# A 31-tap convolution split over three engines, and four FFN tiles per block in another matrix form

## The chip, the cores and the metric

The kernel runs on one core of one Trainium2 chip. Its time is device microseconds of one execution, 2560.61 in the median of three runs before the change (2559.72 to 2563.85). Times in this document are in microseconds (us) unless marked ns. Engines have the profile's names: PE is TensorE (matrix products), DVE is VectorE, ACT is ScalarE, POOL is GpSimd, SP issues the DMAs.

## The reference, cut to what matters

Two residual layers over a sequence of 1024 tokens of width 1024, in float32: a state-space mixer and an FFN, then a causal convolution module and an FFN, then a norm.

```python
def conformer_conv_module(u, w_pw1, b_pw1, dw_w, dw_b, ln_g, ln_b, w_pw2, b_pw2):
    h = u @ w_pw1 + b_pw1
    a, g = jnp.split(h, 2, axis=-1)
    h = a * jax.nn.sigmoid(g)
    h = causal_depthwise_conv(h, dw_w, dw_b)
    h = jax.nn.silu(layernorm(h, ln_g, ln_b))
    return h @ w_pw2 + b_pw2

def swiglu_ffn(u, w_gate, w_up, w_down):
    return (jax.nn.silu(u @ w_gate) * (u @ w_up)) @ w_down
```

The depthwise convolution has 31 taps for each of 1024 channels. An FFN has a hidden width of 2816: 22 tiles of 128.

## The kernel before

Activations stand transposed, 128 channels on the partitions and tokens along the free dimension. The tokens are worked in two blocks of 512, b = 0 and 1. Products are exact to about float32 by splitting each operand: `split` (L200) writes a rounded high half on ACT (L201) and the remainder as a low half on DVE or, where `self.weng` says so, on POOL (L202). `gemm` (L222) then makes three products for each 128 rows of the contraction, low by high, high by low, high by high, 512 columns each (L226). A gate, an up and a pw1 unit contract over 1024, so each is 24 products.

`weight` (L204) brings a unit's weights by one DMA into one of two staging buffers (`wst`) and splits them in two halves of 4 x 128 columns, `whi` and `wlo`, each with four buffers: two units' worth. ACT fills a `whi` when PE has released the one that stood there, and the engine of the low half follows it.

An FFN tile can also be made in the seven-product form (`seven`, L709): the gate (or up) of a pair of tiles is a 2 x 2 block product of which seven instead of eight block products are made, from sums of weight blocks and of activation blocks; each is 4 x 3 products of 256 columns (L758). The sums and the splits are on DVE and ACT.

`run` writes the order of the work as a list of units. Around each block's convolution, a phase goes like this: the norm of the block; then 16 pw1 units (`pw1`, two per tile of 128 channels, one for a and one for g), of which every second ends with a sigmoid on ACT (L946), a gating multiply on DVE (L947) into `ci`, which has 30 columns in front for the tokens before, and in block 0 a copy of the last 30 columns on POOL (L950, the halo of block 1); beside and after them the convolution, one unit per tile (`conv31`); then plain FFN tiles of the other block, in two groups of seven, as matrix work during which the convolution is finished; and, placed between the last of these, the layer norm (`cnorm`) and after it pw2. From the beginning of pw1 to the end of the FFN groups, POOL makes the low halves of the weights (`phase(6, nc.gpsimd)`). The rest of the other block's FFN follows in the seven-product form (`chain7`).

A convolution tile before: one multiply with the bias (L969) and 30 multiply-adds on DVE (L972 in block 0, L974 in block 1), accumulated in a PSUM bank, and in block 0 a copy to SBUF on ACT (L977).

The units' order gives priorities, and a scheduler that runs before the program does makes of it one fixed order of instructions for each engine; `conv31` lowers its own priority by 1000 or 1200, so that its instructions stand behind the units near them. Every engine works its own order strictly from front to back and waits where an operand or a buffer is not ready.

Of the kernel before, what the change touches and what calls it, by code (L numbers as in the profile page):

```python
# [10 lines left out]
AF = mybir.ActivationFunctionType  # L11
ALU = mybir.AluOpType
# [28 lines left out]
BOOST = 60  # L41
NR = 2
HALO = 30
TW = HALO + T
HT = T // 2
MM = 0.2315
# [24 lines left out]
class Unit:  # L71
# [3 lines left out]
    def __init__(self, run, load=None, t=0.0, pre=()):  # L75
        self.run, self.load, self.t, self.pre, self.then = run, load, t, pre, None
# [13 lines left out]
def put(q, *at):  # L90

    out = []
    for i in range(len(q) + 1):
        for k, units in at:
            if (k if k >= 0 else len(q) + k) == i:
                out += units
        out += q[i:i + 1]
    return out


def at(units, places):

    return [(p, units[i:i + 1] if i < len(places) - 1 else units[i:]) for i, p in enumerate(places)]


class Trunk:
# [73 lines left out]
    def halves(self):  # L180
# [4 lines left out]
        self.spare = cp.tile([P, 1], F32, name="spare")  # L185
        self.halo = cp.tile([P, 8, HALO], F32, name="halo")
        o = PAR_OFF["gate"]
# [286 lines left out]
    def in_proj(self, i, u=None, fac=None):  # L474
# [12 lines left out]
        def run(n):  # L487
# [9 lines left out]
            else:  # L497
# [3 lines left out]
                self.nc.scalar.activation(s, acc, AF.Tanh, scale=0.5)  # L501
                self.nc.vector.scalar_tensor_tensor(s, s, 1.0, acc, op0=ALU.add, op1=ALU.mult)
        units = [Unit(lambda n=n: run(n), lambda n=n: load(n)) for n in range(10)]
        if u is not None:
            return [Unit(lambda n=n: gemm(n), lambda n=n: load(n)) for n in range(NR)], [
# [417 lines left out]
    def cin(self, j):  # L923

        return self.ci[j // 3].rearrange("p a t -> p (a t)")[:, j % 3 * TW:(j % 3 + 1) * TW]

    def pw1(self, b):
        nc = self.nc
        W = {}

        def load(j, s):
            W[j, s] = self.weight(self.io["w_pw1"][j, :, s], 8)

        def run(j, s):
            W["acc", s] = self.bank2()
            self.gemm(W["acc", s], W.pop((j, s)), self.U[b])
            if s == 0:
                return
            if j % 3 == 0:
                self.ci.append(self.big.new("ci"))  # L940
            x = self.cin(j)
            dst = x[:, HALO:]
            if b == 1:
                nc.gpsimd.tensor_copy(x[:, :HALO], self.halo[:, j])
            t = self.small.new("sig")
            nc.scalar.activation(t, W.pop(("acc", 1)), AF.Sigmoid, bias=self.pcol("b_pw1", 8 + j))  # L946
            nc.vector.scalar_tensor_tensor(dst, W.pop(("acc", 0)), self.pcol("b_pw1", j), t, op0=ALU.add, op1=ALU.mult)  # L947
            self.small.drop(t)
            if b == 0:
                nc.gpsimd.tensor_copy(self.halo[:, j], x[:, T:])  # L950
            if j == 7:
                self.big.drop(*self.UB.pop(b))
        return [Unit(lambda j=j, s=s: run(j, s), lambda j=j, s=s: load(j, s), 24 * MM)
                for j in range(8) for s in range(2)]

    def conv31(self, b, delay):

        nc, tc = self.nc, self.tc

        def tile_(j):  # L960
            keep = tc.cur_priority
            tc.cur_priority = keep + delay
            if j % 4 == 0:
                self.co[b].append(self.big.new("co"))
            c = self.co[b][j // 4][:, j % 4]
            x = self.cin(j)
            w = lambda s: self.pcol("dw_w", 31 * j + 30 - s)
            acc = self.bank("cv")
            nc.vector.tensor_scalar(acc, x[:, HALO:], w(0), self.pcol("dw_b", j), op0=ALU.mult, op1=ALU.add)  # L969
            for s in range(1, 31):  # L970
                if b == 0:
                    nc.vector.scalar_tensor_tensor(acc[:, s:], x[:, HALO:TW - s], w(s), acc[:, s:], op0=ALU.mult, op1=ALU.add)  # L972
                else:
                    nc.vector.scalar_tensor_tensor(acc if s < 30 else c, x[:, HALO - s:TW - s], w(s), acc,  # L974
                                                   op0=ALU.mult, op1=ALU.add)
            if b == 0:
                nc.scalar.activation(c, acc, AF.Copy)  # L977
            if j == 7:
                self.big.drop(*self.ci)
                self.ci = []  # L980
            tc.cur_priority = keep
        return [Unit(lambda j=j: tile_(j)) for j in range(8)]
# [80 lines left out]
    def run(self):  # L1063
        nc = self.nc
# [40 lines left out]
        fast = lambda *a, **k: self.ffn(*a, fast=True, **k)  # L1105
# [3 lines left out]
        c = self.chain7(fast(0, 0, 6, [0]), fast(0, 6, 6, [0]), fast(0, 12, 4, [0]), fast(0, 16, 2, [0], [0]), free=0, hold=5)  # L1109
        q += [call(self.phase7)] + put(c, *at(n1, (-11, -9, -7, -5, -3))) + [call(self.phase, 8)]  # L1110
        n0 = self.norm_u(0, "cv_norm")
        p1, cv = self.pw1(0), self.conv31(0, 1000)
        c = self.chain(self.ffn(0, 8, 7, [1]), self.ffn(0, 15, 7, [1]))
        q += put(c[:2], *at(n0, (0, 1))) + [call(self.phase, 6, nc.gpsimd)]
        for j in range(8):
            q += p1[2 * j:2 * j + 2] + (cv[j:j + 1] if j < 4 else [])
# [2 lines left out]
        q += [call(self.phase, 8)]  # L1119
        q += put(p2, *at(self.sums_u(1), (2, 3, 4, 5, 6)))  # L1120
        n0 = self.norm_u(0, "ffn_norm", 8)
        c = self.chain7(fast(0, 0, 6, [1]), fast(0, 6, 2, [1], [1]), free=1, hold=6)
        q += [call(self.phase7)] + put(c, *at(n0, (-13, -11, -9, -7, -5))) + [call(self.phase, 8)]
        n1 = self.norm_u(1, "cv_norm")
        p1, cv = self.pw1(1), self.conv31(1, 1200)
        c = self.chain(self.ffn(1, 0, 7, [0]), self.ffn(1, 7, 7, [0]))
        q += put(c[:2], *at(n1, (0, 1))) + [call(self.phase, 6, nc.gpsimd)]
        for j in range(8):
            q += p1[2 * j:2 * j + 2] + (cv[j:j + 1] if j < 4 else [])
# [3 lines left out]
        self.whole = {1}  # L1133
        q += put(p2, *at(self.sums_u(0), (2, 3, 4, 5, 6)))
        n1 = self.norm_u(1, "ffn_norm", 8, whole=True)
        c = self.chain7(fast(1, 14, 6, [0]), fast(1, 20, 2, [0], [0]), free=0, hold=5)
        q += [call(self.phase7)] + put(c, *at(n1, (-13, -11, -9, -7, -5)))
        f0, f1, f2 = self.final(0), self.final(1, (0,)), self.final(1, (HT,))
        c = self.chain7(self.ffn(1, 0, 2, [1]), fast(1, 2, 6, [1]), fast(1, 8, 6, [1]), fast(1, 14, 4, [1]),
                        fast(1, 18, 4, [1], [1], True), free=1, hold=4)  # L1140
# [104 lines left out]
```

## Time and profile before

| | |
|---|---|
| median of three runs | 2560.61 |
| profiled execution: time, span | 2560.45, 2558.7 |
| granted PE clock, mean over the span | 0.995 |
| `wlo` on POOL (L202) | 232 operations, 303.2 busy |
| multiply-adds of the convolution, L972 and the larger group of L974 | 240 and 232, 160.1 and 158.6 busy |
| block 0: first gating multiply, last multiply-add | 1224.2, 1445.3 |
| block 1: first multiply-add, last | 1727.5, 1949.1 |

A row of the time line has start, length, engine, line, operation, what it writes and reads, and in brackets how long the engine was idle before it and on whom it waited. A row by stretch of time has, for each engine, its busy time and in parentheses the number of its instructions. A row of one line's instructions has the shortest, median and longest duration in ns. A PE product is shown longer than the time after which the next one starts.

### The profile page before, as it was taken

How to read it: one execution, taken by the hardware profiler on the slowest of the kernel's cores; microseconds unless marked ns; L12 is line 12 of the kernel's file. 1: busy time of each engine (PE TensorE's matmuls, PEld its weight loads, DVE VectorE, ACT ScalarE, POOL GpSimd, SP SyncE). 2: the span in 40 equal slices, each digit the busy share in tenths (PEclk: the TensorE clock that was granted, in tenths of full speed). 3: DMA queues.
4: the chain of work that ended last, by engine and by line, in shares of the span. 5: the costliest groups of instructions: out<-in, count | busy, mean ns of one | idle time of the engine just before them, and what ended most of it. 6: DMA issues, size and time to landing. Idle time of an engine off the chain costs nothing. (4 is left out here: it accounts for less than half of the span.)

```text
span 2558.7 us, 35973 instructions
## 1 busy us (share of the span) xinstructions
PE 2516.8 (98%) x13794; PEld 2132.0 (83%) x13794; DVE 2066.5 (81%) x3158; ACT 1224.7 (48%) x2135; POOL 473.7 (19%) x449
## 2 busy tenths in 40 slices
PE   8999999999999999998999999999999999999998
PEld 6787887888887899997888879978888899799997
DVE  7898889888889886768899677589996776996676
ACT  5554565655555454544333364452323554554443
POOL 3213211111111000000544540004444300000000
PEclk9999999999999999999999999999999999999999
DMA  4222222222223223322232333222233322332322
GB/s 144 82 65 74 78 61 75 75 79 71 75 71 103 84 104 100 107 72 79 91 99 91 98 125 103 65 86 94 99 91 97 127 88 88 128 120 93 114 85 71
DMA packets 72316, 233.54 MB, mean 91 GB/s; under 512 B 8016, under 2 KB 14416, under 8 KB 65232
## 3 DMA queue, kind: packets, MB, share of 16 engines
q1 hardware_dynamic: 72144, 231.25, 27.9%
q8 instruction: 108, 1.77, 0.3%
q14 instruction: 64, 0.52, 0.1%
HBM read 227.02 MB, written 4.19 MB: 90 GB/s over the span
## 5 line engine op out<-in xcount | busy, mean ns | idle before, releaser
L201 ACT ACTIVATE whi<-wst 128x512 fp32r<-128x512 f32 (+3 forms) x676 | 402.8, 597 | 815.4 <-PE p L226 657.8
L226 PE MATMUL p<-uhi_b,wlo 128*128 128x512 f32 x1432 | 572.1, 400 | 4.5 <-DVE wlo L202 2.3
L226 PE MATMUL p<-ulo_b,whi 128*128 128x512 f32 x1432 | 562.2, 393 | 3.0 <-DVE ulo_b L202 2.1
L226 PE MATMUL p<-uhi_b,whi 128*128 128x512 f32 x1432 | 562.6, 393 | 0.0
L202 POOL TENSOR_TENSOR wlo<-wst,whi 128x512 fp32r<-128x512 f32 x232 | 303.2, 1308 | 761.0 <-ACT whi L201 760.7
L226 PE MATMUL p<-hid_b,whi 128*128 128x512 f32 x1344 | 420.0, 393 | 2.3 <-DVE hid_b L202 2.3
L202 DVE TENSOR_TENSOR wlo<-wst,whi 128x512 fp32r<-128x512 f32 (+2 forms) x444 | 303.1, 685 | 136.9 <-ACT whi L201 133.5
L226 PEld LDWEIGHTS p<-uhi_b,wlo 128*128 128x128 f32 x1432 | 269.4, 188 | 70.0 <-ACT uhi_b L201 3.8
L226 PEld LDWEIGHTS p<-ulo_b,whi 128*128 128x128 f32 x1432 | 269.4, 188 | 66.5 <-DVE ulo_b L202 3.9
L758 PE MATMUL p<-uhi_b,wh_b 128*128 128x256 f32 x1728 | 322.0, 281 | 0.4 <-DVE wh_b L202 0.4
L226 PEld LDWEIGHTS p<-uhi_b,whi 128*128 128x128 f32 x1432 | 269.3, 188 | 60.4 <-issue 0.2
L226 PEld LDWEIGHTS p<-hid_b,whi 128*128 128x128 f32 x1344 | 252.4, 188 | 57.6 <-DVE hid_b L202 3.2
L758 PEld LDWEIGHTS p<-uhi_b,wh_b 128*128 128x128 f32 x1728 | 272.6, 189 | 2.6 <-DVE wh_b L202 0.6
L226 PE MATMUL p<-hid_b,wlo 128*128 128x512 f32 x672 | 265.7, 395 | 2.4 <-DVE h L862 2.2
L758 PE MATMUL p<-ulo_b,wh_b 128*128 128x256 f32 x864 | 243.0, 282 | 0.0
L758 PE MATMUL p<-tu_b,wh_b 128*128 128x256 f32 x1296 | 170.4, 281 | 0.0
L758 PEld LDWEIGHTS p<-ulo_b,wh_b 128*128 128x128 f32 x864 | 163.7, 190 | 1.9
L758 PEld LDWEIGHTS p<-tu_b,wh_b 128*128 128x128 f32 x1296 | 161.3, 189 | 0.8
L972 DVE SCALAR_TENSOR_TENSOR p<-ci_b,par,p 128x503 f32<-128x503 f32 (+28 forms) x240 | 160.1, 734 | 0.6
L974 DVE SCALAR_TENSOR_TENSOR p<-ci_b,par,p 128x512 f32<-128x512 f32 x232 | 158.6, 748 | 0.5
L201 ACT ACTIVATE wh_b<-ws_b 128x1024 fp32r<-128x1024 f32 x108 | 114.0, 1059 | 87.6 <-PE p L758 37.7
L226 PEld LDWEIGHTS p<-hid_b,wlo 128*128 128x128 f32 x672 | 126.3, 188 | 31.8 <-DVE h L862 4.6
(235 smaller groups left out, 3984.7 us busy)
## 6 DMA issues: line engine op xcount, KB each, us to landing
wq_b<-w_gu SPq DMA_DIRECT2D x54, 1024.0 KB, 4.8
wst<-w_in SPq DMA_DIRECT2D x80, 512.0 KB, 3.5
wst<-w_gu SPq DMA_DIRECT2D x68, 512.0 KB, 3.5
wst<-w_pw SPq DMA_DIRECT2D x48, 512.0 KB, 3.5
wst<-w_dn SPq DMA_DIRECT2D x48, 384.0 KB, 3.1
wst<-w_out SPq DMA_DIRECT2D x64, 256.0 KB, 2.6
wst<-w_dn SPq DMA_DIRECT2D x32, 448.0 KB, 3.3
wst<-w_dn SPq DMA_DIRECT2D x32, 256.0 KB, 2.7
```

The costliest lines, as they stand in the source:

```text
L201: self.nc.scalar.activation(hi, src, AF.Copy)
L202: (eng or self.nc.vector).tensor_tensor(lo, src, hi.bitcast(F32), ALU.subtract)
L226: self.nc.tensor.matmul(acc, a, b, start=n == 0, stop=n == tot - 1)
L758: nc.tensor.matmul(to, x, y, start=n == 0 and not more, stop=n == 11, skip_group_check=True)
L972: nc.vector.scalar_tensor_tensor(acc[:, s:], x[:, HALO:TW - s], w(s), acc[:, s:], op0=ALU.mult, op1=ALU.add)
L974: nc.vector.scalar_tensor_tensor(acc if s < 30 else c, x[:, HALO - s:TW - s], w(s), acc, op0=ALU.mult, op1=ALU.add)
```

## The change

Of a tile's 31 taps, 22 stay on DVE (1 to 22, into PSUM). Tap 0 with the bias becomes an Identity on ACT into the SBUF tile `co`, the remaining eight become scaled copies on ACT into a half-size buffer (`ct`, two places in turn), and POOL adds each to `co` in place. At the end DVE adds its PSUM sum to `co`. In block 0 the first 30 columns of each `ci` are now cleared by POOL instead of being left out.

The FFN tiles beside each convolution become two groups of five instead of two of seven. The four tiles left over join the seven-product part, which gets a further group.

```diff
+NTAP = 23
...
             if b == 1:
                 nc.gpsimd.tensor_copy(x[:, :HALO], self.halo[:, j])
+            else:
+                nc.gpsimd.memset(x[:, :HALO], 0.0)
...
-            nc.vector.tensor_scalar(acc, x[:, HALO:], w(0), self.pcol("dw_b", j), op0=ALU.mult, op1=ALU.add)
-            for s in range(1, 31):
-                if b == 0:
-                    nc.vector.scalar_tensor_tensor(acc[:, s:], x[:, HALO:TW - s], w(s), acc[:, s:], op0=ALU.mult, op1=ALU.add)
-                else:
-                    nc.vector.scalar_tensor_tensor(acc if s < 30 else c, x[:, HALO - s:TW - s], w(s), acc,
-                                                   op0=ALU.mult, op1=ALU.add)
-            if b == 0:
-                nc.scalar.activation(c, acc, AF.Copy)
+            old = lambda k: k if b == 0 else 0
+            nc.vector.tensor_scalar(acc, x[:, HALO - 1:TW - 1], w(1), None, op0=ALU.mult)
+            for k in range(2, NTAP):
+                o = old(k)
+                nc.vector.scalar_tensor_tensor(acc[:, o:], x[:, HALO - k + o:TW - k], w(k), acc[:, o:],
+                                               op0=ALU.mult, op1=ALU.add)
+
+            nc.scalar.activation(c, x[:, HALO:], AF.Identity, scale=w(0), bias=self.pcol("dw_b", j))
+            tmp = self.half.new("ct")
+            for k in range(NTAP, 31):
+                o = old(k)
+                t = tmp.rearrange("p (i a) c -> p i (a c)", i=2)[:, k % 2, o:]
+                nc.scalar.activation(t, x[:, HALO - k + o:TW - k], AF.Copy, scale=w(k))
+                nc.gpsimd.tensor_tensor(c[:, o:], c[:, o:], t, ALU.add)
+            self.half.drop(tmp)
+            nc.vector.tensor_tensor(c, c, acc, ALU.add)
...
-        c = self.chain(self.ffn(0, 8, 7, [1]), self.ffn(0, 15, 7, [1]))
+        c = self.chain(self.ffn(0, 12, 5, [1]), self.ffn(0, 17, 5, [1]))
...
-        c = self.chain7(fast(0, 0, 6, [1]), fast(0, 6, 2, [1], [1]), free=1, hold=6)
+        c = self.chain7(fast(0, 0, 6, [1]), fast(0, 6, 4, [1]), fast(0, 10, 2, [1], [1]), free=1, hold=6)
...
-        c = self.chain(self.ffn(1, 0, 7, [0]), self.ffn(1, 7, 7, [0]))
+        c = self.chain(self.ffn(1, 0, 5, [0]), self.ffn(1, 5, 5, [0]))
...
-        c = self.chain7(fast(1, 14, 6, [0]), fast(1, 20, 2, [0], [0]), free=0, hold=5)
+        c = self.chain7(fast(1, 10, 6, [0]), fast(1, 16, 4, [0]), fast(1, 20, 2, [0], [0]), free=0, hold=5)
```

How the order on the engines changes. POOL, the beginning of block 0's pw1 units, before (`wlo` are the low halves of the weights, `halo` the copies for block 1):

```order
L202 TENSOR_TENSOR wlo_1390_11197<-wst_1388_11194,whi_1389_11196 128x512
L950 COPY halo_174<-ci_b172_11120 128x30
L202 TENSOR_TENSOR wlo_1392_11201<-wst_1388_11194,whi_1391_11200 128x512
L202 TENSOR_TENSOR wlo_1396_11236<-wst_1394_11233,whi_1395_11235 128x512
L202 TENSOR_TENSOR wlo_1398_11240<-wst_1394_11233,whi_1397_11239 128x512
```

The same place now; `co` is the convolution's tile, `ct` the products:

```order
L953 COPY halo_174<-ci_b172_11120 128x30
L985 TENSOR_TENSOR co_b173_11136<-co_b173_11136,ct_x19_11161 128x489
L985 TENSOR_TENSOR co_b173_11136<-co_b173_11136,ct_x19_11161 128x488
L985 TENSOR_TENSOR co_b173_11136<-co_b173_11136,ct_x19_11161 128x487
L203 TENSOR_TENSOR wlo_1392_11211<-wst_1388_11204,whi_1391_11210 128x512
L985 TENSOR_TENSOR co_b173_11136<-co_b173_11136,ct_x19_11161 128x486
L985 TENSOR_TENSOR co_b173_11136<-co_b173_11136,ct_x19_11161 128x485
L985 TENSOR_TENSOR co_b173_11136<-co_b173_11136,ct_x19_11161 128x484
L203 TENSOR_TENSOR wlo_1396_11247<-wst_1394_11244,whi_1395_11246 128x512
L985 TENSOR_TENSOR co_b173_11136<-co_b173_11136,ct_x19_11161 128x483
L985 TENSOR_TENSOR co_b173_11136<-co_b173_11136,ct_x19_11161 128x482
L203 TENSOR_TENSOR wlo_1398_11251<-wst_1394_11244,whi_1397_11250 128x512
```

The eight additions of the first tile stand between the splits of the next two units. The other seven tiles of block 0 follow in the same way, one for every two units, so that between the first of the 64 additions and the last there are 30 splits; from the second tile on, four additions come before the second split, three before the third and one before the fourth. In block 1 it is 64 additions and 31 splits. After them the order is splits alone again.

ACT, the second tile of block 0: the sigmoid and the high halves of the weights (`whi`) before,

```order
L946 ACTIVATE sig_s232_11229<-p3_1393_11204,par_66 128x512
L201 ACTIVATE whi_1402_11303<-wst_1401_11301 128x512
L201 ACTIVATE whi_1404_11307<-wst_1401_11301 128x512
L201 ACTIVATE whi_1408_11342<-wst_1407_11340 128x512
L201 ACTIVATE whi_1410_11346<-wst_1407_11340 128x512
```

and now:

```order
L979 ACTIVATE co_b173_11136<-ci_b172_11120,par_66 128x512
L202 ACTIVATE whi_1402_11323<-wst_1401_11321 128x512
L984 ACTIVATE ct_x20_11278<-ci_b172_11120,par_66 128x489
L984 ACTIVATE ct_x20_11278<-ci_b172_11120,par_66 128x488
L984 ACTIVATE ct_x20_11278<-ci_b172_11120,par_66 128x487
L984 ACTIVATE ct_x20_11278<-ci_b172_11120,par_66 128x486
L202 ACTIVATE whi_1404_11327<-wst_1401_11321 128x512
L984 ACTIVATE ct_x20_11278<-ci_b172_11120,par_66 128x485
L984 ACTIVATE ct_x20_11278<-ci_b172_11120,par_66 128x484
L984 ACTIVATE ct_x20_11278<-ci_b172_11120,par_66 128x483
L202 ACTIVATE whi_1408_11363<-wst_1407_11361 128x512
L984 ACTIVATE ct_x20_11278<-ci_b172_11120,par_66 128x482
```

The Identity and the products of the tile came in between the high halves, in the places where POOL has the additions. From the third product on, each waits until POOL has added the one before the last, whose buffer it takes.

## The prediction

> **What bounds the kernel now.** I read the page first, then the busy time by stretch around the convolution, then TensorE's waits there and GpSimd's instructions in order of time. The page's first lines:
>
> ```profile
> span 2558.7 us, 35973 instructions
> PE 2516.8 (98%) x13794; PEld 2132.0 (83%) x13794; DVE 2066.5 (81%) x3158; ACT 1224.7 (48%) x2135; POOL 473.7 (19%) x449
> ```
>
> TensorE has work for 98% of the span. The next view gives busy time by stretch: block 0's pw1 units, the rest of its convolution, and block 1's pw1 units.
>
> ```profile
> core 0: us, PE busy (x) PEld busy (x) DVE busy (x) ACT busy (x) POOL busy (x), PEclk, DMA share, GB/s
> 1223.40:1300.60 77.20, 77.20 (x338) 63.30 (x338) 70.24 (x106) 23.50 (x39) 37.85 (x36) 1.00 0.30 96
> 1300.60:1480.00 179.40, 179.40 (x778) 145.81 (x777) 145.95 (x206) 62.05 (x104) 86.64 (x68) 1.00 0.31 96
> 1723.00:1800.00 77.00, 77.00 (x336) 62.77 (x335) 68.45 (x102) 23.15 (x36) 36.60 (x29) 1.00 0.31 103
> ```
>
> TensorE never pauses there; GpSimd is half busy. Its work is the low halves of the weights (wlo): half a gemm's weights each. All that TensorE waited for it in block 0's phase:
>
> ```profile
> PE p L226 <- POOL wlo L202: 0.4, 1, 0.4
> ```
>
> GpSimd's order of time, and one ScalarE row that released its first:
>
> ```profile
> 1225.11 1.30 POOL L202 TENSOR_TENSOR wlo<-wst,whi 128x512 fp32r<-128x512 f32 x1 [1.53 <-ACT whi L201]
> 1226.34 0.22 POOL L950 COPY halo<-ci_b 128x30 f32<-128x30 f32 x1
> 1227.84 1.29 POOL L202 TENSOR_TENSOR wlo<-wst,whi 128x512 fp32r<-128x512 f32 x1 [1.28 <-ACT whi L201]
> 1230.60 1.30 POOL L202 TENSOR_TENSOR wlo<-wst,whi 128x512 fp32r<-128x512 f32 x1 [1.47 <-ACT whi L201]
> 1233.33 1.29 POOL L202 TENSOR_TENSOR wlo<-wst,whi 128x512 fp32r<-128x512 f32 x1 [1.43 <-ACT whi L201]
> ```
> ```profile
> 1224.40 0.63 ACT L201 ACTIVATE whi<-wst 128x512 fp32r<-128x512 f32 x1 [0.19 <-PE p L226]
> ```
>
> A split takes 1.29 and the next comes 2.75 later (1227.84, 1230.60, 1233.33), which is TensorE's time for half a gemm; so TensorE sets the pace and GpSimd has 1.46 free per half. TensorE releases a weight buffer at about 1224.3; four buffers hold half a gemm each, so what fills it is needed three halves (8.3) later, at 1232.6, and is there at 1226.4: a lead of 6.2. Everything below turns on that lead and those 1.46.
>
> **The change: matrix work.** Eight FFN tiles (four per block) leave the plain form: 8 x 2 gate/up x 24 = 384 products of 512 columns. They come back as four pairs x 2 x 7 x 12 = 672 of 256 columns. Prices from a stretch with 512-column products alone and one with both, the second followed by L758 (the 256-column ones) by itself:
>
> ```profile
> 1024.00:1152.00 128.00, 128.00 (x905) 119.97 (x904) 90.71 (x126) 59.47 (x92) 0.00 (x0) 1.00 0.27 89
> 1280.00:1408.00 128.00, 128.00 (x557) 104.38 (x556) 117.96 (x182) 41.90 (x70) 61.30 (x50) 1.00 0.30 95
> ```
> ```profile
> 1024.00:1152.00 128.00, 86.81 (x719) 86.56 (x718) 1.00 0.27 89
> ```
>
> 512 columns: 128/557 = 0.2298. 256 columns: (128 - (905 - 719) x 0.2298)/719 = 0.1186. So 384 x 0.2298 = 88.2 go, 672 x 0.1186 = 79.7 come: 8.5 less. The seven-product stretch has TensorE at 128 of 128 with VectorE at 91, so the form's extra VectorE sums stay hidden; if that cover went, they would show there. The down products are as many as before; one more group per block adds eight accumulations to VectorE, also hidden.
>
> **VectorE** drops from 31 multiply-adds a tile to 22 plus one final addition. It was not what TensorE waited for, so this gains nothing directly. It only lets the phase be four FFN tiles shorter:
>
> ```profile
> 1245.52 9.71 DVE L972 SCALAR_TENSOR_TENSOR p<-ci_b,par,p 128x494 f32<-128x494 f32 x15
> ```
>
> At 9.71/15 = 0.65 a tile costs 22 x 0.65 + 0.8 + 0.7 + 0.75 = 16.5, eight 132, which end well inside the shorter phase.
>
> **ScalarE** gains one Identity and eight scaled copies a tile. It loses block 0's copy out of PSUM. The nearest rows are an Identity with two per-partition operands, a copy with one, and the sigmoid:
>
> ```profile
> L467 ACT ACTIVATE v_s<-sf_b x48: 800/814/832, 51.9 to 746.0; 128x512 f32<-128x512 f32 x48
> ```
> ```profile
> L334 ACT ACTIVATE rhi_b<-h,par x8: 705/708/721, 5.6 to 16.2; 128x512 fp32r<-128x512 f32 x8
> ```
> ```profile
> L946 ACT ACTIVATE sig_s<-p,par x16: 669/670/689, 1223.5 to 1801.1; 128x512 f32<-128x512 f32 x16
> ```
>
> Per tile: four high halves 2.5, 8 x 0.7 = 5.6, 0.81, 0.67: 9.6. Two product buffers let it run two ahead of GpSimd; a product (0.7) is shorter than an addition, so ScalarE follows and does not lead.
>
> **GpSimd** gains 8 additions a tile. They are no free filler: it works in order, and the order above puts all eight of a tile between the four splits of that tile's two gemms. The next split is queued behind them, and TensorE waits for it. An addition of two tiles in place is L247; a narrower operation shows the slope:
>
> ```profile
> L202 POOL TENSOR_TENSOR wlo<-wst,whi x232: 1009/1293/2282, 1215.4 to 2025.4; 128x512 fp32r<-128x512 f32 x116
> ```
> ```profile
> L247 POOL TENSOR_TENSOR ssum_s<-ssum_s,sq_s x10: 1292/1529/1830, 10.2 to 261.7; 128x512 f32<-128x512 f32 x10
> ```
> ```profile
> 247.18 1.04 POOL L237 TENSOR_TENSOR sq_s<-h 128x512 f32<-128x512 f32 x1
> 248.18 2.67 POOL L247 TENSOR_TENSOR ssum_s<-ssum_s,sq_s 128x512 f32<-128x512 f32 x2
> ```
> ```profile
> 1395.93 1.02 POOL L202 TENSOR_TENSOR wlo<-wst,whi 128x384 fp32r<-128x384 f32 x1 [0.69 <-ACT whi L201]
> 1398.79 1.30 POOL L202 TENSOR_TENSOR wlo<-wst,whi 128x512 fp32r<-128x512 f32 x1 [1.84 <-ACT whi L201]
> ```
>
> 512 wide costs 1.293 undisturbed; 0.28 per 128 columns makes block 0's 482 to 489 columns 1.235; block 1's are 512. Two chained additions took 2.67, so one that waits for the one before loses another 0.08. Below, 1.04 (L237, one operand read twice) is the least any 512-wide two-operand row shows; above, 1.53 is L247's median with VectorE reading two SBUF tiles. I take 1.235 and 1.293: the multiply-adds beside it read one operand from PSUM, and the splits beside them keep 1.29.
>
> The Trainium skill speaks against the move: GPSIMD Engine Reference, section 4.1, sends ordinary elementwise additions to VectorE, and section 3.1 gives about 2.6 cycles per element at 1.2 GHz. An estimate from that page is 1.05 for 485 columns and 1.11 for 512; the sum would then come to about 2594. The rows above have a little more, and they decide.
>
> Now the sum. Count from the first addition, about 1226.5, when the latest split done is the one TensorE needs at 1232.6; the next is needed at 1235.4, 8.9 later.
> Block 0, to the split after the last addition: 64 x 1.235 = 79.0, 41 chained x 0.08 = 3.3, 31 splits x 1.29 = 40.0, 7 halo copies x 0.29 = 2.0: 124.3. TensorE asks for that split after 8.9 + 30 x 2.76 = 91.7. Late by 32.6.
> Block 1: 64 x 1.293 = 82.8, 40 x 0.08 = 3.2, 32 x 1.29 = 41.3: 127.3, against 8.9 + 31 x 2.76 = 94.5. Late by 32.8.
> Afterwards GpSimd has half its time free again, but TensorE has no slack elsewhere in which to win it back. Total: -8.5 + 32.6 + 32.8 = +56.9, a span of 2615.6. The profiled execution took 2560.45 (its span and 1.75 around it), the median of the three is 2560.61: **2617**. Without the 0.08 it is 2611.
>
> Can GpSimd itself wait for TensorE, which would make it worse? From the half that ends a tile's gemms, the way to its first addition is 2.8 + sigmoid 0.67 + gating 0.75 + Identity 0.81 + a high half 0.63 + a product 0.7 and some 0.5 of hand-overs, 6.9; by the order GpSimd has 3 additions, a split, an addition, a split, a halo copy and a split before it, 9.3. So no, with 2.4 to spare.
>
> **The rivals.**
> *Faster: GpSimd keeps up.* Its splits in block 0's phase were
>
> ```profile
> 1223.40:1300.60 77.20, 0.00 (x0) 36.45 (x29) 1.00 0.30 96
> 1300.60:1480.00 179.40, 12.30 (x13) 86.43 (x67) 1.00 0.31 96
> ```
>
> 122.9 of 256.6. With 85 of additions that fits a phase of some 240, if spread over it: then only -8.5 is left, 2552. It decides where 31 splits, the copies and 64 additions fit into 91.7: an addition of 0.73. Against it: no row has less than 1.04, and the order packs them into the first third. 6%, and 2% for about no change.
>
> *A smaller loss.* Additions at 1.04: 64 x 0.985 in block 0 and 64 x 1.04 in block 1 make each 16.6 late, 2585. 8%.
>
> *A larger one: the clock.* A tile's four splits end 6.5 (four additions and a split), 5.2 (three), 2.5 (one) and 1.6 (a halo copy) after each other, 15.8 in all, and TensorE works 2.76 after each: it idles 4.7, in two stops of some 2.4. A stop before block 1's convolution, then what was granted:
>
> ```profile
> 1710.39 0.72 PE L226 MATMUL p<-ulo_b,whi 128*128 128x512 f32 x1 [1.49 <-DVE ulo_b L202]
> ```
> ```profile
> 1707.08:1710.49 3.41, 1.80 (x8) 0.93 (x6) 3.37 (x6) 2.73 (x5) 0.00 (x0) 1.00 0.00 0
> 1710.49:1713.90 3.41, 3.41 (x9) 2.63 (x10) 3.41 (x6) 3.07 (x5) 0.00 (x0) 0.50 0.51 154
> ```
>
> A stop of 1.49 was followed by 3.41 at half clock, 1.7 of work lost. I expect this about once a tile; the idle 4.7 and the 2.4 to spare on the way above cover it, so it costs nothing. If that cover is thinner than I reckon, 16 x 1.7 = 27 come on top: 2644. 12%. The Trainium skill (TensorE: Matmul & The Clock Gate, "What's actually happening") lets the clock fall only after an idle window of about 3.4 us, which no stop here would fill; the trace has it after less.
>
> **How the numbers follow.** The forecast keeps 72%. Its own bounds are 2611 and, with a few splits slowed beside VectorE, about 2625. The range reaches into the larger loss and part of the smaller, 2596 to 2648. A measurement can tell about 0.2% (5) from no change: faster 6%, same 2%, slower 92%.
>
> **What would show it.** GpSimd near 100% busy from 1226 to about 1350, and again in block 1; TensorE waiting for wlo from GpSimd some 60 in all, in stops of 1 to 4, and nowhere else more than now; the additions 128 times at 1.2 to 1.3; clock dips in these two stretches only; after them TensorE full again. Wrong, if TensorE stays full through pw1, if the additions take under 1.1, or if the wait sits on ScalarE's products or behind the convolution's end instead.

## The result and the profile after

The changed kernel takes **2624.53 us** in the median of four runs (2620.99 to 2625.69); the kernel before took 2560.45 beside it (2559.72 to 2563.85). The ratio is 1.0243, with a 95% interval of 1.0231 to 1.0255: slower, by 64 us. Forecast were 2617 and a range of 2596 to 2648.

The page's first lines of the changed kernel, to be laid beside those of before:

```profile
span 2619.1 us, 36905 instructions
PE 2529.7 (97%) x14082; PEld 2149.3 (82%) x14082; DVE 2058.7 (79%) x3138; ACT 1335.1 (51%) x2307; POOL 580.9 (22%) x553
```

GpSimd has only 107 us more work and is still at 22% of the span, but the span grew by 60.4. The view by stretch of time shows where, with the same columns as before: the pw1 units of block 0 up to 1300.6 as before, the rest of GpSimd's additions there, the remainder of the convolution, and the pw1 units of block 1.

```profile
1223.40:1300.60 77.20, 63.88 (x258) 49.77 (x257) 50.97 (x77) 46.23 (x74) 73.63 (x66) 0.96 0.20 69
1300.60:1345.00 44.40, 37.91 (x153) 29.61 (x154) 29.11 (x45) 26.94 (x44) 43.25 (x38) 0.96 0.21 71
1345.00:1480.00 135.00, 132.28 (x575) 106.84 (x574) 112.02 (x154) 54.15 (x95) 74.42 (x61) 1.00 0.30 90
1754.00:1862.00 108.00, 89.83 (x351) 68.66 (x349) 70.11 (x105) 63.68 (x99) 103.87 (x83) 0.94 0.21 69
```

The last busy time before the clock is GpSimd's. It was 37.85 of 77.20 and is 73.63 now, then 43.25 of 44.40; TensorE, which was full, made 258 products in the first stretch where it made 338. From 1345 on GpSimd has half its time free again. The same happens in block 1. What TensorE waited for from 1223.4 to 1350, in one row where 0.4 stood before, and GpSimd's instructions in order of time at the start of that:

```profile
PE p L227 <- POOL wlo L203: 21.9, 11, 3.3
```
```profile
1226.75 3.90 POOL L985 TENSOR_TENSOR co_b<-co_b,ct_x 128x489 f32<-128x489 f32 x3
1230.60 1.31 POOL L203 TENSOR_TENSOR wlo<-wst,whi 128x512 fp32r<-128x512 f32 x1
1231.85 3.87 POOL L985 TENSOR_TENSOR co_b<-co_b,ct_x 128x486 f32<-128x486 f32 x3
1235.68 1.29 POOL L203 TENSOR_TENSOR wlo<-wst,whi 128x512 fp32r<-128x512 f32 x1
...
1242.08 5.19 POOL L985 TENSOR_TENSOR co_b<-co_b,ct_x 128x489 f32<-128x489 f32 x4
1247.22 1.27 POOL L203 TENSOR_TENSOR wlo<-wst,whi 128x512 fp32r<-128x512 f32 x1
```

No row of these has a bracket for idle time: one instruction follows the other, and a split that TensorE needs every 2.76 us comes 5.1 us after the last. The additions by themselves, with who waited for them:

```profile
L985 POOL TENSOR_TENSOR co_b<-co_b,ct_x x128: 1202/1262/1312, 1226.8 to 1879.2; 128x512 f32<-128x512 f32 x64, 128x489 f32<-128x489 f32 x8, 128x488 f32<-128x488 f32 x8, 128x487 f32<-128x487 f32 x8
...
  ACT ct_x L984: 82.5, 65
```

ScalarE's products wait for GpSimd, 82.5 us in all, and not the other way round. A second, smaller loss lies where the prediction expected none: at the end of the runs of seven-product tiles, the larger part after the second convolution. The experiments below call such a place a seam. TensorE's waits from 2062 to 2560, and VectorE's order of time at the worst of them:

```profile
PE p L227 <- DVE h L863: 6.6, 3, 3.1
```
```profile
2249.57 0.69 DVE L248 TENSOR_TENSOR ssum_s<-ssum_s,sq_s 128x512 f32<-128x512 f32 x1
2250.17 0.74 DVE L318 SCALAR_TENSOR_TENSOR ru_b<-h,par,p 128x512 f32<-128x512 f32 x1
2250.88 0.69 DVE L203 TENSOR_TENSOR wlo<-wst,whi 128x512 fp32r<-128x512 f32 x1
2251.49 0.69 DVE L248 TENSOR_TENSOR ssum_s<-ssum_s,sq_s 128x512 f32<-128x512 f32 x1
2252.09 0.69 DVE L203 TENSOR_TENSOR ulo_b<-ru_b,uhi_b 128x512 fp32r<-128x512 f32 x1
2252.69 0.69 DVE L203 TENSOR_TENSOR wlo<-wst,whi 128x512 fp32r<-128x512 f32 x1
2253.29 0.69 DVE L203 TENSOR_TENSOR ulo_b<-ru_b,uhi_b 128x512 fp32r<-128x512 f32 x1
2253.89 1.88 DVE L863 TENSOR_TENSOR h<-h,p 128x512 f32<-128x512 f32 x3
```

VectorE works without a pause on the norm of the next phase while TensorE waits 3.1 us for the accumulation (L863) of the last down products.

To compare kernels, the span is cut at a few events of the trace: the first and the eighth gating multiply of each block (L947, now L950) and the first and last pw2 product. A and D: first to eighth gating, block 0 and 1. B and E: from there to pw2. C: pw2 of block 0 to the first gating of block 1. F: pw2 of block 1 to the end. The four plain tiles that the change takes out of B and of E are 4 x 72 x 0.2298 = 66.2 each; as four tiles of the other form they bring 4 x 84 x 0.1186 + 96 x 0.2298 = 61.9 (the first term their gates and ups, the second their down products) into C and F.

| kernel | first gating | A | B | C | D | E | F |
|---|---|---|---|---|---|---|---|
| before | 1224.2 | 75.6 | 222.4 | 158.9 | 76.0 | 223.1 | 489.4 |
| after | 1224.5 | 104.6 | 157.8 | 223.1 | 106.9 | 156.9 | 556.7 |
| after less before, regrouping taken out | +0.3 | +29.0 | +1.6 | +2.3 | +30.9 | 0 | +5.4 |

With 8.6 less for the cheaper form (2 x (61.9 - 66.2)) the differences make 60.9, against 60.4 of the spans (the two pw2 are some tenths shorter). Block 0 loses 30.6, A and B together, block 1 30.9, and 7.7 come in C and F.

### The profile page after: what moved, and what is told of

Read it like the earlier page. It is cut to its first block, busy times and chain, and to the rows that moved or that the text cites. A ratio compares the mean times of both kernels' runs of the same rounds, so it can differ in the third digit from the quotient of the medians.

```text
span 2619.1 us, 36905 instructions
## 1 busy us (share of the span) xinstructions
PE 2529.7 (97%) x14082; PEld 2149.3 (82%) x14082; DVE 2058.7 (79%) x3138; ACT 1335.1 (51%) x2307; POOL 580.9 (22%) x553
## 4 chain that ended last, share of the span: by engine, by line
PE 79%; DVE 8%; POOL 7%; issue 3%; ACT 2%; DMA 1%; SPq 0%; DVEq 0%; ACTq 0%; POOLq 0%
PE p L227 50%; PE p L759 23%; POOL co_b L985 5%; POOL wlo L203 2%; DVE wlo L203 1%; PE p L593 1%; PE p L597 1%; PE p L585 1%; DVE ssum_s L248 1%; PE p L262 1%; DVE v_s L470 1%; DVE un_s L318 1%; DVE ulo_b L203 1%; ACT whi L202 1%; PE p L549 0%
## 5 line engine op out<-in xcount | busy, mean ns | idle before, releaser
L202 ACT ACTIVATE whi<-wst 128x512 fp32r<-128x512 f32 (+2 forms) x660 | 383.6, 584 | 606.7 <-PE p L227 510.5
L227 PE MATMUL p<-uhi_b,wlo 128*128 128x512 f32 x1304 | 530.5, 408 | 46.9 <-POOL wlo L203 41.8
L227 PE MATMUL p<-ulo_b,whi 128*128 128x512 f32 x1304 | 518.2, 398 | 2.6 <-DVE ulo_b L203 1.4
L227 PE MATMUL p<-uhi_b,whi 128*128 128x512 f32 x1304 | 517.4, 397 | 0.0
L759 PE MATMUL p<-uhi_b,wh_b 128*128 128x256 f32 x1984 | 370.1, 282 | 0.4 <-DVE wh_b L203 0.4
L759 PEld LDWEIGHTS p<-uhi_b,wh_b 128*128 128x128 f32 x1984 | 313.4, 190 | 3.1 <-DVE wh_b L203 0.6
L203 POOL TENSOR_TENSOR wlo<-wst,whi 128x512 fp32r<-128x512 f32 x200 | 251.4, 1269 | 238.6 <-ACT whi L202 238.6
L227 PEld LDWEIGHTS p<-ulo_b,whi 128*128 128x128 f32 x1304 | 249.0, 191 | 60.9 <-DVE ulo_b L203 3.2
L976 DVE SCALAR_TENSOR_TENSOR p<-ci_b,par,p 128x512 f32<-128x512 f32 (+18 forms) x336 | 229.5, 741 | 1.2
L203 DVE TENSOR_TENSOR wh_b<-ws_b,wh_b 128x1024 fp32r<-128x1024 f32 x124 | 150.9, 1222 | 27.6 <-ACT wh_b L202 27.0
L985 POOL TENSOR_TENSOR co_b<-co_b,ct_x 128x512 f32<-128x512 f32 (+8 forms) x128 | 161.6, 1263 | 6.5
```

Of the source, the lines that this page charges most:

```text
L202: self.nc.scalar.activation(hi, src, AF.Copy)
L203: (eng or self.nc.vector).tensor_tensor(lo, src, hi.bitcast(F32), ALU.subtract)
L227: self.nc.tensor.matmul(acc, a, b, start=n == 0, stop=n == tot - 1)
L759: nc.tensor.matmul(to, x, y, start=n == 0 and not more, stop=n == 11, skip_group_check=True)
L976: nc.vector.scalar_tensor_tensor(acc[:, o:], x[:, HALO - k + o:TW - k], w(k), acc[:, o:], op0=ALU.mult, op1=ALU.add)
L985: nc.gpsimd.tensor_tensor(c[:, o:], c[:, o:], t, ALU.add)
```

## The experiments

Theory A: GpSimd's additions stand ahead of the weight splits on a queue that works in order, and TensorE waits. The main rival, B: the loss comes from taking cover away (matrix work that hides the other engines' work), the four plain tiles a block that stood beside the convolution. Others are taken up as they came. The stretches of all kernels, as above:

| kernel | first gating | A | B | C | D | E | F | median | ratio to before |
|---|---|---|---|---|---|---|---|---|---|
| split convolution alone | 1224.4 | 104.7 | 223.6 | 159.0 | 106.9 | 223.2 | 490.2 | 2623.54 | 1.024 (1.0225 to 1.0256) |
| regrouping alone | 1225.7 | 75.6 | 169.0 | 223.1 | 76.6 | 175.8 | 558.4 | 2601.83 | 1.0153 (1.0139 to 1.0166) |
| 27 steps on VectorE | 1226.6 | 75.5 | 158.5 | 223.2 | 77.5 | 160.6 | 557.9 | 2570.44 | 1.003 (1.0019 to 1.0042) |
| two groups of six | 1224.6 | 104.6 | 159.4 | 214.4 | 106.9 | 157.6 | 546.9 | 2606.52 | 1.0171 (1.0157 to 1.0185) |
| 25 steps | 1225.8 | 86.5 | 156.0 | 224.3 | 89.2 | 154.9 | 557.0 | 2583.59 | 1.0091 (1.0075 to 1.0108) |
| 27 steps, two of six | 1224.1 | 75.5 | 158.4 | 214.4 | 77.8 | 159.8 | 546.9 | 2549.78 | 0.9962 (0.9949 to 0.9975) |
| additions on VectorE | 1228.2 | 78.2 | 167.8 | 222.9 | 78.2 | 175.2 | 558.5 | 2599.82 | 1.0156 (1.0141 to 1.017) |
| before, four and four | 1224.2 | 75.6 | 222.4 | 152.7 | 76.2 | 223.3 | 484.7 | 2551.0 | 0.9966 (0.9953 to 0.9978) |
| 27 steps, sixes everywhere | 1214.9 | 75.9 | 158.7 | 214.8 | 77.2 | 160.0 | 546.7 | 2538.47 | 0.9911 (0.9897 to 0.9924) |
| before, no group of two | 1215.4 | 75.0 | 222.6 | 152.9 | 76.2 | 222.8 | 485.3 | 2540.61 | 0.9916 (0.9903 to 0.993) |

**The two halves of the change, each alone.** The split convolution with the old groups:

```diff
-        c = self.chain(self.ffn(0, 12, 5, [1]), self.ffn(0, 17, 5, [1]))
+        c = self.chain(self.ffn(0, 8, 7, [1]), self.ffn(0, 15, 7, [1]))
...
-        c = self.chain7(fast(0, 0, 6, [1]), fast(0, 6, 4, [1]), fast(0, 10, 2, [1], [1]), free=1, hold=6)
+        c = self.chain7(fast(0, 0, 6, [1]), fast(0, 6, 2, [1], [1]), free=1, hold=6)
```

(block 1 in the same way).

> The new convolution split (nine steps as ScalarE products that GpSimd adds) with the old grouping of the FFN tiles: seven and seven plain ones beside it, six and two in the seven-product form. Theory A (GpSimd's additions stand ahead of the weight splits on its in-order queue, so TensorE waits while the first eight tiles are gated, whatever stands beside the convolution later): the stretch from the first to the eighth gating stays at about 105 us in both blocks, where the kernel before had 76, and the time is 2560.5 + 30.6 + 30.9 = about 2622 us. Theory B (the loss is that four plain tiles a block were taken away from beside the convolution, so that something there runs out of cover): with the old grouping back the time is within a few microseconds of 2560.5. The half-clock theory C (the clock that falls at each stop is what costs, not the stop) expects the same as A here and does not part from it.

2623.54. A and D are those of the changed kernel to a tenth, and TensorE's waits from 1223 to 1350 are the same row:

```profile
PE p L227 <- POOL wlo L203: 21.9, 11, 3.3
```

With all fourteen tiles back in B and E, nothing of the loss is won back: theory B falls as the cause of it, and the claim that TensorE has no slack later in which to make up a delay holds. Now the other half, the kernel before with the new groups alone (the lines marked + in the change's last four hunks).

> The kernel before with nothing but the new grouping of the FFN tiles (five and five plain ones beside the convolution, six, four and two in the seven-product form); all 31 steps stay on VectorE. Theory A: no addition stands on GpSimd, so the gating stretches stay at 76 us. What comes instead is VectorE's: it was busy for 178.7 of the 222.0 us from the eighth gating to the second pointwise product; four tiles fewer take some 9 us from it and 66 us from the stretch, so it needs about 170 us where 156 are left and is late by 14 or more a block. Sum 2560.5 - 8.6 (cheaper form) + 7.9 (the seams of the additional group, 2.4 and 5.5 in the changed kernel) + 28 = about 2588 us, with 2575 to 2600 as the reach. Theory B (missing cover is the whole loss of the changed kernel): 2615 us or more, since here too the four tiles are gone. If the time came out below 2560, VectorE had more room than its busy share shows.

2601.83, above the expected reach by 2: A and D stay at 76, as A said. But the loss in B and E is more than the 14 each of the estimate. The two stretches, B and E:

```profile
1301.30:1470.30 169.00, 159.20 (x680) 127.35 (x678) 155.59 (x231) 64.58 (x111) 79.80 (x70) 0.98 0.31 96
1818.10:1993.90 175.80, 161.55 (x679) 129.53 (x677) 162.74 (x235) 61.68 (x105) 81.67 (x69) 0.96 0.31 93
```

VectorE is at 155.59 of 169.00 and at 162.74 of 175.80, GpSimd at about half. Against 222.4 - 66.2 = 156.2 and 156.9, B and E are 12.8 and 18.9 late, pw2 lasts some 3 longer each (48.1 and 47.6 from its first to its last product, where it was 44.7 and 44.4), and C and F have their seams, 2.3 and 7.1. So what theory B names exists: with 31 steps a tile on VectorE (its operations for one tile: the taps that it keeps, and where there is one the final addition) the shorter phase costs 12.8 + 18.9 + 3.4 + 3.2, some 38 us. The split convolution removes just that, and puts a larger loss in its place.

**Fewer additions.** One number is changed, `NTAP`, 23 in the changed kernel: 27 leaves four additions a tile on GpSimd, 25 leaves six.

```diff
-NTAP = 23
+NTAP = 27
```

> The changed kernel with 27 steps left on VectorE instead of 23 (so five ScalarE products and four GpSimd additions a tile instead of nine and eight). Theory A: 32 additions a block instead of 64 take 32 x 1.30 = 41.6 us from GpSimd's queue, more than the 30.6 and 30.9 us of delay, so the gating stretches go back to 76 us, with single stops of 1 to 2 us at most, and the time is 2624.5 - 61.5 = about 2563 us, give or take 6, or up to 15 more if VectorE, which then has 32 more steps of 0.73 us a block, is late at the layer norm. Theory B (missing cover): the FFN grouping is that of the changed kernel, so the time stays at about 2620. Theory C (the half clock costs, at a like number of stops): stops at half the length, half of the loss left, about 2593.

2570.44, within the reach. A is 75.5, and from 1226 to 1350 no wait of TensorE is left. GpSimd's order of time at its start, and the row of stretch A:

```profile
1228.86 3.87 POOL L985 TENSOR_TENSOR co_b<-co_b,ct_x 128x485 f32<-128x485 f32 x3
1232.68 1.31 POOL L203 TENSOR_TENSOR wlo<-wst,whi 128x512 fp32r<-128x512 f32 x1
1233.93 1.24 POOL L985 TENSOR_TENSOR co_b<-co_b,ct_x 128x482 f32<-128x482 f32 x1
1235.12 2.56 POOL L203 TENSOR_TENSOR wlo<-wst,whi 128x512 fp32r<-128x512 f32 x2
1237.61 0.21 POOL L953 COPY halo<-ci_b 128x30 f32<-128x30 f32 x1
1238.39 1.30 POOL L203 TENSOR_TENSOR wlo<-wst,whi 128x512 fp32r<-128x512 f32 x1 [0.56 <-ACT whi L202]
```
```profile
1226.60:1302.10 75.50, 75.50 (x332) 61.95 (x331) 69.45 (x106) 44.01 (x70) 67.38 (x61) 1.00 0.28 91
```

At 1238.39 GpSimd waits for ScalarE again, so it has caught up; TensorE is full, 75.50 of 75.50, with GpSimd at 67.38. B and E are 2.3 and 3.7 late. TensorE's waits there, 2.1 and 2.9 in all, are for the halves of an FFN's hidden tile (`hid_b`); that VectorE's four more steps a tile make these late is likely, but not shown. The first gating came 2.4 later than before, in work that no edit touched: such differences of the program's start, up to 4 us, are scatter of the single profile.

> The changed kernel with 25 steps left on VectorE: six GpSimd additions a tile, 48 a block, between the eight of the changed kernel and the four of the kernel with 27 steps. Theory A (the delay is GpSimd's whole queue against a fixed cover of some 86 us): 16 additions fewer at 1.30 us take 20.8 us from each block's delay of 30.6 and 30.9, about 10 are left, the gating stretches last about 86 us, and the time is 2624.5 - 41.6 = about 2583 us. A theory of a price for each addition (every addition delays TensorE by the same share, 30.75 / 64 = 0.48 us) gives delays of 23 a block and about 2609 us.

2583.59. A price for each addition would have given 2609; a queue with a fixed cover, the time before TensorE asks for the split behind the last addition, gave 2583 and fits to a microsecond in the total, though A and D, 10.9 and 13.2 late, are some 2 apart. The stretch, and the waits from 1226 to 1350:

```profile
1225.80:1312.30 86.50, 80.28 (x342) 63.18 (x341) 68.88 (x105) 52.67 (x84) 83.53 (x74) 1.00 0.24 80
```
```profile
PE p L227 <- POOL wlo L203: 7.4, 10, 1.5
```

The prediction's sum can be set against three kernels here. GpSimd's time is from its first addition to the end of the split after the last, the cover 8.9 + 2.76 for each split but the first:

| | GpSimd, block 0 and 1 | cover | late by the sum | measured (A, D against before) |
|---|---|---|---|---|
| 64 additions | 121.3, 125.1 | 91.7, 94.5 | 29.6, 30.6 | 29.0, 30.9 |
| 48 | 101.3, 102.9 | 91.7, 91.7 | 9.6, 11.2 | 10.9, 13.2 |
| 32 | 86.8, 89.8 | 88.9, 88.9 | none, 0.9 | none, 1.5 |

The first two rows test the sum. In the last one 8.8 and 10.9 of GpSimd's time are waits of its own, so it says no more than that there is room.

**Additions on VectorE.** The products stay on ScalarE; only the engine that adds them is another.

```diff
-                nc.gpsimd.tensor_tensor(c[:, o:], c[:, o:], t, ALU.add)
+                nc.vector.tensor_tensor(c[:, o:], c[:, o:], t, ALU.add)
```

> The changed kernel with the nine ScalarE products kept and the eight additions a tile done by VectorE instead of GpSimd. Theory A (GpSimd's queue): the gating stretches go back to about 76 us, although ScalarE does the same products. VectorE then has 64 additions of some 0.7 us a block, nearly what the 72 steps weighed, so it is late at the layer norm as in the kernel with the new grouping alone (12.8 and 18.9 us there): about 2595 us, reach 2585 to 2605. Rival D (ScalarE's products, which stand in line with the gatings and the high halves of the weights, are what delays TensorE): the gating stretches stay near 105 us and the time at 2620 or above.

2599.82. A and B, by stretch:

```profile
1228.20:1306.40 78.20, 78.20 (x343) 64.19 (x342) 78.02 (x111) 44.45 (x73) 38.91 (x35) 1.00 0.30 97
1306.40:1474.20 167.80, 157.16 (x667) 124.69 (x666) 165.56 (x233) 84.35 (x146) 87.57 (x69) 0.99 0.29 88
```

In A TensorE is full again with the same products on ScalarE (44.45 busy, 46.23 to 1300.6 in the changed kernel): rival D falls. The load has moved to VectorE, 78.02 of 78.20 and 165.56 of 167.80, and B and E are 11.6 and 18.3 late, much as with the regrouping alone. An addition that met no split of GpSimd took 0.66 us here, as expected; but most met one and took longer (last section): the 64 of a block add up to 58 and 61 us, not to the 42 that this price would make. That is 16 and 19 us more, about as much as B and E are late; whether VectorE would be in time without it was not tried. The Trainium skill (GPSIMD Engine Reference, section 4.1) sends such additions to VectorE. The trace agrees: 0.66 us against 1.24 to 1.29 on GpSimd, and the kernel is 25 us better than with GpSimd's queue, though 40 worse than the kernel before.

**The seams.** The twelve tiles in two groups instead of three, in the changed kernel; block 1 alike.

```diff
-        c = self.chain7(fast(0, 0, 6, [1]), fast(0, 6, 4, [1]), fast(0, 10, 2, [1], [1]), free=1, hold=6)
+        c = self.chain7(fast(0, 0, 6, [1]), fast(0, 6, 6, [1], [1]), free=1, hold=6)
```

> The changed kernel with the twelve tiles of the seven-product form in two groups of six and six instead of three of six, four and two; the number of products is the same. Theory A2 (the 2.4 and 5.5 us that the stretches of this form took beyond their products are the seams of the additional group, where TensorE waits for VectorE's accumulation and loses its clock once): 7 to 8 us less, about 2617 us. Rival A3 (they are spread over the products, or come from the order of the weight splits): no change that can be measured, 2622 to 2627.

2606.52: 18 less, not 7 or 8. A and D stay; C falls by 8.7 and F by 9.8, and not one wait for L863 is left in them. A2 had the place right and the size wrong: C and F are now 6.4 and 4.4 shorter than what the kernel before would have with four more tiles (158.9 + 61.9, 489.4 + 61.9). So the kernel before paid for a seam as well. Its waits from 1567 to 1726:

```profile
PE p L226 <- DVE h L862: 1.7, 2, 1.5
PE p L226 <- DVE ulo_b L202: 1.5, 1, 1.5
```

A test of that on the kernel before, which keeps the number of groups and changes only their size:

```diff
-        c = self.chain7(fast(0, 0, 6, [1]), fast(0, 6, 2, [1], [1]), free=1, hold=6)
+        c = self.chain7(fast(0, 0, 4, [1]), fast(0, 4, 4, [1], [1]), free=1, hold=6)
```

> The kernel before with its eight tiles of the seven-product form as four and four instead of six and two; nothing else. Theory A2, made narrower by the kernel with two groups of six (a group of two tiles gives TensorE 6 products a down-projection unit, 1.38 us, against one accumulation of 0.68 us and one weight split of 0.66 on VectorE, so VectorE runs behind and TensorE waits): the kernel before pays for its own group of two as well, and gains 6 to 10 us: 2552 to 2557. Rival A3 (only the third group cost something, the group of two is free): no change, 2560 to 2564.

2551.0, a microsecond below what was expected: C 6.2 less, F 4.7 less, everything else the same to three tenths. With the number of groups unchanged, it is the group of two at the end of a run that lets VectorE fall behind. What stands ahead of it counts as well: a group of four between the six and the two cost the changed kernel 2.3 and 5.4 more. The run of eighteen tiles below, as three groups of six, leaves no wait for an accumulation, so more groups alone do not do it.

How VectorE falls behind is not the balance of one down unit that the expectation names. In the changed kernel, from 2230 to 2254, around TensorE's stops, VectorE's time went among others to these:

```profile
L318 DVE SCALAR_TENSOR_TENSOR ru_b<-h,par,p 128x512 f32<-128x512 f32 x8 | 5.8, 742 | 0.0
L203 DVE TENSOR_TENSOR ulo_b<-ru_b,uhi_b 128x512 fp32r<-128x512 f32 x8 | 5.4, 688 | 0.5 <-ACT uhi_b L202 0.4
L863 DVE TENSOR_TENSOR h<-h,p 128x512 f32<-128x512 f32 x8 | 5.4, 681 | 0.0
L203 DVE TENSOR_TENSOR wlo<-wst,whi 128x256 fp32r<-128x256 f32 x8 | 3.4, 420 | 0.0
```

An accumulation and a split of 256 columns are 1.10 us a unit, less than the 1.38 of TensorE's six products. But the norm of the next phase (the first two rows, 11.2) stands between them in VectorE's order. Shown are the place, the wait, this work in between and the wait's disappearance. That a larger last group helps because it gives TensorE more products beside the norm (a group of two has 48, 11 us) is argued.

**Versions built from this.** 27 steps and two groups of six:

> 27 steps on VectorE (four GpSimd additions a tile) together with the seven-product tiles in two groups of six: the two repairs at once. The first alone gave 2570.4 us, the second took 18.0 us (2624.5 to 2606.5). If they add up, 2552 to 2553 us, which is 0.4% faster than the kernel before at 2562.6. If the stops that the second removes only moved the layer norm's start, so that VectorE becomes late at 27 steps, about 2560.

2549.78, where 2552 to 2553 was expected: the two repairs add up. Then the same for the run of eighteen tiles ahead of the first convolution:

```diff
-        c = self.chain7(fast(0, 0, 6, [0]), fast(0, 6, 6, [0]), fast(0, 12, 4, [0]), fast(0, 16, 2, [0], [0]), free=0, hold=5)
+        c = self.chain7(fast(0, 0, 6, [0]), fast(0, 6, 6, [0]), fast(0, 12, 6, [0], [0]), free=0, hold=5)
```

> The kernel with 27 steps and two groups of six, and in addition the first long run of seven-product tiles (eighteen in block 0, ahead of the first convolution) as six, six and six instead of six, six, four and two. Theory A2 (a last group of two leaves VectorE behind, wherever it stands): the stretch from 1163 us to the first gating at 1224 us gets shorter, since the layer norm there starts from accumulations that come later than they could; by the 6.3 us that the same edit gave ahead of the second convolution, about 2543 to 2545 us in all. Rival: there TensorE waited for the accumulations of the small group only 0.5 us in the trace, and the stops that it has (2.3 us for the norm's diagonal and 1.5 us for the halves of its first tile) stay: 2548 to 2551 us.

2538.47, better than either expected: the rival was wrong that those stops stay, and A2 put their price too low. With the group of two the last stretch before the first gating was, first row, and in it a piece at half clock, second row:

```profile
1162.80:1224.10 61.30, 55.05 (x228) 42.58 (x227) 49.59 (x92) 33.07 (x55) 5.13 (x4) 0.92 0.24 77
1202.45:1212.69 10.24, 6.59 (x13) 4.33 (x14) 9.18 (x20) 6.18 (x9) 0.00 (x0) 0.50 0.15 51
```

Without it:

```profile
1159.00:1212.70 53.70, 53.70 (x240) 43.90 (x239) 40.28 (x71) 28.04 (x50) 3.91 (x3) 1.00 0.31 94
```

This window ends 2.2 us before the first gating; up to there TensorE stays full. The stops (61.30 - 55.05 = 6.3) and the half clock both go. At half clock TensorE was busy for 6.59, of which half is lost, 3.3: together 9.6, and the first gating comes 9.2 earlier. The two profiled executions differ by 8.4 (2547.46 and 2539.06), the medians by 11.3; what makes up the rest is not known. Last, the kernel before, its convolution untouched, with no group of two:

> The kernel before, with its own convolution (all 31 steps on VectorE), and nothing changed but the groups of the seven-product form: four and four instead of six and two, and six, six and six instead of six, six, four and two. If the groups explain all that the better versions gained, 2551.0 - 11.3 (2549.8 to 2538.5, what the second edit gave beside the split convolution) = about 2540 us, so that splitting the convolution at 27 steps brings nothing by itself that can be measured. If the split convolution brings a part of it, 2545 or more here against 2538.5 there.

2540.61. Beside 2538.47 their intervals overlap: the split convolution at 27 steps brings nothing that can be measured. All that the best versions gained, 0.9%, is to be had from the groups alone.

## Why the prediction was right, and where not

*Matrix work, -8.5.* Held: the page has 288 products more (13794 to 14082), which is 672 less 384. Kernels without a group of two give the price apart from the seams: C and F of "two groups of six" are 61.7 and 62.2 longer than those of "before, four and four", for four tiles reckoned at 61.9; and B and E of the split alone are 65.8 and 66.3 longer than those of the changed kernel, reckoned at 66.2.

*GpSimd, +32.6 and +32.8.* The mechanism is shown by four kernels (split alone, 27, 25, additions on VectorE). The price was exact: additions took 1.235 in block 0 and 1.292 in block 1 (medians), as forecast from the split's 1.293 and the slope with the width, and one that waits for the one before starts 1.315 after it in block 0, the 0.08 included. The term was a little too large all the same: it measured 30.6 and 30.9. GpSimd needed 121.3 where 124.3 was forecast, since an instruction that does not wait for the one before starts a little ahead of its end: some 1.19 after an addition, 1.24 after a split (1230.60 to 1231.85), where 1.235 and 1.29 were reckoned, and 0.16 after a halo copy instead of 0.29. By the figure of the Trainium skill (GPSIMD Engine Reference, section 3.1) the estimate for the whole was 2594, some 30 below what was measured.

*"One more group per block adds eight accumulations to VectorE, also hidden."* This step failed. It rested on the mean of VectorE over the seven-product stretch (91 of 128), but at a run's last group VectorE has no time free at all (from 2247.5 to 2257.7, around the longest wait, it is busy throughout). It cost 2.3 in C and 5.4 in F, and the group of two that the kernel before had already costs 6.2 and 4.7.

*The sum.* -8.6 + 30.6 + 30.9 + 7.7 = 60.6, where 56.9 was forecast. Two errors of opposite sign, 3.9 too much and 7.7 too little, leave some 4: that the forecast came this near is in part luck. The profiled execution took 2620.99, 4 above 2617; it was the shortest of the four, and their median lies 3.5 higher.

*VectorE's shorter convolution.* That it "gains nothing directly" holds, but its price had to be told: without it the shorter phase costs some 38.

*The clock.* It dips in the two stretches, as forecast, though three times in block 0's convolution and five windows in block 1's, not sixteen, and one more comes at the seam in F, which "in these two stretches only" excluded. Whether a dip costs by itself was left at 12%. 25 steps answers: no half clock in its A and D, and its lateness follows the same sum. In the changed kernel the half clock is a part of the delay that GpSimd sets, not an addition: TensorE's 41.8 of waits (forecast some 60), and half of the 26.0 for which it was busy in eight windows of 3.41 at half clock, 13.0, make 54.8 of the 61.5. The other 6.7 are not traced to a cause.

*The rivals.* "GpSimd keeps up" needed additions under 0.73; they took 1.26. Spreading them over the phase was not tried. "A smaller loss" fell with the additions' time too: no addition took less than 1.20.

## What to carry to other kernels

An engine's share of the span says nothing of its room: before work is put on an engine that others wait for, lay its order beside the pace at which they consume, and sum what stands ahead of each needed result; here 48 additions a block were 11 and 13 us too many, where 32 delayed TensorE by 1.5 at most. A price "hidden beside a busy neighbour" is to be checked at the end of a run, where groups are small and the next phase's work begins, not against the mean of the stretch. When two edits come together, run each alone: here each was slower alone, and the only gain lay in the sizes of the last groups, which the change had left at two.

## What the runs showed of the hardware

The half clock comes after windows in which TensorE was not idle. Three windows in a row and then two more of the changed kernel, 3.41 us each on the grid in which the clock changed:

```profile
1247.37:1250.79 3.42, 2.24 (x10) 1.86 (x11) 0.68 (x2) 1.70 (x3) 3.34 (x3) 1.00 0.35 114
1250.79:1254.20 3.41, 1.41 (x7) 0.86 (x6) 1.35 (x3) 2.50 (x5) 3.33 (x4) 1.00 0.10 40
1254.20:1257.61 3.41, 3.41 (x10) 2.67 (x9) 3.41 (x7) 1.96 (x4) 3.41 (x5) 0.50 0.16 48
...
1322.47:1325.88 3.41, 1.76 (x9) 1.12 (x8) 1.22 (x2) 1.21 (x2) 3.41 (x3) 1.00 0.04 10
1325.88:1329.29 3.41, 1.97 (x9) 1.30 (x7) 0.15 (x1) 3.02 (x5) 3.25 (x4) 1.00 0.37 144
```

After a window with seven products, 1.41 busy, the next is at half clock; after one with nine, 1.76, it is not. From 1214 to 2600 in this kernel, every window at full clock with at most 1.46 busy was followed by half clock and none with 1.70 or more; in the kernel before one with 1.80 was and one with 1.67 was not, so the line lies about there and the modelled busy time does not give it exactly. The Trainium skill (TensorE: Matmul & The Clock Gate, "What's actually happening") asks for an idle window; here one that is two fifths busy is enough.

An addition of two SBUF tiles on VectorE and a split on GpSimd scarcely overlap: the one that begins later ends as if it had waited for the other. Two of each, from the kernel with the additions on VectorE:

```profile
1231.78 0.66 DVE L985 TENSOR_TENSOR co_b<-co_b,ct_x 128x488 f32<-128x488 f32 x1
1231.84 1.76 POOL L203 TENSOR_TENSOR wlo<-wst,whi 128x512 fp32r<-128x512 f32 x1 [1.28 <-ACT whi L202]
1234.60 1.30 POOL L203 TENSOR_TENSOR wlo<-wst,whi 128x512 fp32r<-128x512 f32 x1 [1.00 <-ACT whi L202]
1234.70 1.72 DVE L985 TENSOR_TENSOR co_b<-co_b,ct_x 128x486 f32<-128x486 f32 x1
```

The first split began just after an addition and ended 1.16 after that one's end; the second addition began just after a split and ended 0.52 after the split's end. So it is throughout. Of 64 additions that began while a split ran, 62 ended 0.52 to 0.62 after it; the other two, begun within 0.05 of the split, went first. The 22 splits of 512 columns that began while an addition ran ended 1.14 to 1.20 after that. Additions that met no split took 664 ns in the median, those that met one 1125. The multiply-adds beside the splits, with one operand in PSUM, do not show this: in the kernel before, the splits beside them keep their 1.29.
